# Weight sums in place, PSUM bank pairs by role and a later gate in a two-layer transformer block on one Trainium2 core

## The chip, the core and the metric

The kernel runs on one core of one Trainium2 chip. The metric is the device time of the whole program in microseconds. The engines are named as in the profile: PE (TensorE, with PEld for its weight loads), DVE (VectorE, "Vector"), ACT (ScalarE), POOL (GpSimd) and SP (SyncE, which issues the transfers).

## What is computed

The reference runs two layers on 256 tokens of width 1024. Each layer has a feed-forward block, a mixer and a second feed-forward block; a norm ends the program. So four feed-forward blocks run in all, and the change lies in them and in the first mixer.

```python
def swiglu(x, w_gate, w_up, w_down):          # 1024 -> 2816 -> 1024
    return (jax.nn.silu(x @ w_gate) * (x @ w_up)) @ w_down
...
for layer in range(DEPTH):                     # DEPTH = 2
    x = x + 0.5 * swiglu(rms_norm(x, ffn_norm[layer, 0]), ...)
    h = rms_norm(x, mix_norm[layer])
    x = x + (hybrid_ab_mixer(h, ...) if layer % 2 == 0 else short_conv_mixer(h, ...))
    x = x + 0.5 * swiglu(rms_norm(x, ffn_norm[layer, 1]), ...)
return rms_norm(x, final_norm)
```

All data are float32. The hybrid mixer (layer 0) has a gated unit and causal attention with four heads; the other is a short convolution.

## The kernel before

Precision is kept by splitting every weight and every activation into a rounded high part and a low rest (whi and wlo, hi and lo). A product is three matmuls: high by high, and the two mixed ones.

**The weight stream.** The class `Weights` holds the list of weight chunks (`Item`s) in the order of use. Sync loads a chunk into one of five raw slots (L71). ACT writes whi (`high`, L95), Vector writes wlo = raw - whi (`low`, L100); each has four buffers. `low` also returns the raw slots that an item drops and starts the next loads. An item may ask for sums of raw chunks first, which Vector computes (`sums`, L91). `next`, called once per chunk by the code of the matmuls, runs `catch_up`: high parts are issued three chunks ahead, low parts two, and sums one further than the high parts. Each engine works its own list strictly in the order in which the code issues it, so an instruction that waits holds up all behind it.

**A feed-forward block** (`ffn`). First a pair of 256 columns of gate and up is "opened" (`open_pairs`, transposed output, banks named by `ps()`); ACT and Vector take it out of PSUM (`added`, L418 and L424, tiles ev_g and ev_u). In block 1 the pair is opened by code of its own. Then 26 steps follow, one per chunk, in the order of the string `ORDER`; I number them from 0. "n" is a step of a plain unit: 512 columns of gate and up, four chunks, 24 matmuls each; gate goes to one pair of banks, up to another, then silu (L545) and the product v (`times`, L542). "s" is a step of a sum unit: 12 matmuls. A sum unit computes the two products of 512 columns for both token halves with seven half-size products instead of eight, from sums of the weight chunks b11, b12, b21, b22 and sums of activations (`Sums.make`, tiles xs and xp). Plain steps are 0, 1, 3, 5, 7, 10, 12, 14, 16, 18, 21 and 25. The results v (or r of a sum unit) are turned by four PE transposes each (`turned`, L533) into one misc bank and split into hx (L405 on ACT, L408 on Vector); the second turn of a unit uses the same bank as the first, so it waits for the first one's hx. Between the steps hooks run: the norm's column matmuls (L372), ten small Vector operations from rs_v (L309) to diag (L377), the broadcast matmul (L382, rbc) and the gate of the opened pair (`gated`, L430, L522, L523, hx). After the loop come the down products (L282, L284). In block 4 they are natural products into `ps(0)`.

**PSUM.** There are three pairs of banks, ps0 to ps2 (`ps`), and two single banks (`misc`). `ps()` takes the next pair in turn. In the block's loop the pairs are fixed: gate ps1, up ps2, sum units ps0. Which pairs the opened products hold depends on the turn: ps1 and ps2 in blocks 1 and 4, ps0 and ps1 in blocks 2 and 3.

**Sum unit before.** Its seven items are, in order: b11; t = b11 - b12, with t in a raw slot that loads nothing; b11 = b11 - (b12 + b22), with both sums asked for by this item; b22; b12 + b22; b21; b11 + b21. In the program that is four sums in three places. In the loop's order the sums are issued in steps 0, 2 (two of them) and 9, and for the second unit in steps 13, 15 (two) and 20.

**Block 1's hooks.** Step 8 loads small tensors, step 15 computes the angles (15 small Vector operations, L686 to L706), step 22 computes sines and then `turn_small`: the gains' transpose (L257), Vector's copy of it (gains_mix, L259) and four transposes of w_s (L731) into the same bank.

Of the kernel before, what the change touches and what calls it, by code (L numbers as in the profile page):

```python
# [10 lines left out]
F32 = mybir.dt.float32  # L11
# [36 lines left out]
class Weights:  # L48
# [6 lines left out]
    def __init__(self, nc, pool, items):  # L55
        self.nc, self.pool, self.items = nc, pool, items
        self.src = [load for item in items for load in item.loads]
        self.shapes = {name: tuple(src.shape) for name, src in self.src if src is not None}
        self.loaded = self.summed = self.highs = self.lows = self.used = 0
        self.raw, self.parts, self.queue = {}, {}, []  # L60
        self.free = [f"raw{i}" for i in range(RAW_BUFS)]

    def load_piece(self, i, s, e):
        name, src = self.src[i]
        if name not in self.raw:
            tag = self.free.pop(0)
            shape = list(src.shape) if src is not None else [P, 4, 512]
            self.raw[name] = self.pool.tile(shape, F32, tag=tag, bufs=1, name="raw"), tag
            self.loaded = i + 1
        if src is not None:  # L70
            self.nc.sync.dma_start(self.raw[name][0][:, s:e], src[:, s:e])  # L71

    def load(self):
        while self.loaded < len(self.src) and self.free:
            src = self.src[self.loaded][1]
            self.load_piece(self.loaded, 0, 0 if src is None else src.shape[1])

# [58 lines left out]
def block_kernel(ctx: ExitStack, tc: tile.TileContext, a, out):  # L136
# [35 lines left out]
    def sum_unit(g, u, c):  # L172

        b11, b12, b21, b22, t = (next(names) for _ in range(5))
        lo, hi = slice(0, 4), slice(4, 8)
        yield Item([(b11, u[:, lo, c])], b11, drop=[])
        yield Item([(b12, g[:, lo, c]), (t, None)], t, [(t, b11, b12, ALU.subtract)])
        yield Item([(b22, g[:, hi, c])], b11, [(b12, b12, b22, ALU.add), (b11, b11, b12, ALU.subtract)], drop=[])
        yield Item([], b22)
        yield Item([], b12)  # L180
        yield Item([(b21, u[:, hi, c])], b21, drop=[])
        yield Item([], b11, [(b11, b11, b21, ALU.add)], drop=[b11, b21])
# [259 lines left out]

    def open_pairs(xs, order=range(KB), mm=mm_t, banks=None):

        tiles = [(W.next(later=i > 0), ps(banks and banks[i])) for i in range(2)]
        W.flush(W.used + 1)
# [4 lines left out]

    def t_pair(xs, mid=None, mm=None, i=None):
        w, p = W.next(), ps(i)
        for b in range(2):
# [8 lines left out]

    def out_projection(h, norm, order, banks=None):
        ys = open_pairs(h, order, banks=banks)
        W.catch_up()
# [44 lines left out]
    def ffn(norm, nxt, hooks=None, opened=None, squares=None):  # L511
# [57 lines left out]
        def summed(f):  # L569

            p, b = ps(0), misc(0)
            a, c = p[:, 0], p[:, 1]
# [45 lines left out]
        g0, u0 = (added(p, tag) for p, tag in zip(pairs, ("ev_g", "ev_u")))  # L618
        W.catch_up()
        steps = {"n": (i for j in (0, 2, 4) for i in plain(2 + 4 * j)),  # L620
                 "s": (i for j in (1, 3) for i in summed(2 + 4 * j))}

        def scale():
            norm.broadcast()
            gated(g0, u0)

        if opened:
            head = {0: [squares, xs.gained], 1: [norm.column, lambda: xs.make(0)], 2: [scale], 3: [lambda: xs.make(1)]}
        else:
            head = {0: [norm.column], 1: [scale]}  # L630
        head[5], head[6] = [lambda: xs.make(2)], [lambda: xs.make(3)]
# [94 lines left out]
    def turn_small():  # L726

        small["turn"]()
        wp = misc(1)
# [76 lines left out]
    norm = nxt  # L806


    def project(i, mid=None):
        p = ps(i)  # L810
        for c in range(2):
# [29 lines left out]
    def heads_t(xs, name, i):  # L841
        r, p = big(name), ps(i)
        for t, x in enumerate(xs):
# [34 lines left out]
    def scores():  # L878
        s0p, s1p = misc(), ps(1)
        pr0, pr1 = big("prob0"), big("prob1")  # L880
# [40 lines left out]

    u_ps = t_pair(norm.x, scores, mm_s, 0)
    u0 = gate(u_ps)
    normalize()
    v_ps = project(2)
    v_sb = scaled(v_ps, "v")
# [8 lines left out]
    for c in range(2):  # L935
        nc.vector.tensor_copy(pt_a[c][:, :, :P], p[:, c * S:(c + 1) * S].rearrange("p (h k) -> p h k", h=2))
    p = ps(0)
    for c in range(2):
# [10 lines left out]
    def mix():  # L949

        ms, m_ps = big("mixed"), ps(2)
        for c in range(2):
# [210 lines left out]
```

## Time and profile before

| what | us |
|---|---|
| median of 3 runs | 976.96 (976.76 to 978.97) |
| profiled execution | 977.29 |
| its span | 975.5 |
| mean granted PE clock, share of full | 0.986 |
| PE busy | 933.1 |
| DVE busy | 729.3 |
| ACT busy | 504.2 |
| the four loops of steps, from their first matmul | 20.8 to 152.0, 315.5 to 430.6, 506.8 to 621.3, 790.1 to 907.3 |

The times of the profile are microseconds from the start of the span, which is the time from the first to the last instruction. The profiled execution's own time holds the span and what lies around it. In a row of waits the numbers are the total, how often and the longest. In a row of the timeline they are start and length; a bracket gives the engine's idle time ahead of it and what ended it.

### The profile page before, as it was taken

How to read it: one execution, taken by the hardware profiler on the slowest of the kernel's cores; microseconds unless marked ns; L12 is line 12 of the kernel's file. 1: busy time of each engine (PE TensorE's matmuls, PEld its weight loads, DVE VectorE, ACT ScalarE, POOL GpSimd, SP SyncE). 2: the span in 40 equal slices, each digit the busy share in tenths (PEclk: the TensorE clock that was granted, in tenths of full speed). 3: DMA queues.
4: the chain of work that ended last, by engine and by line, in shares of the span. 5: the costliest groups of instructions: out<-in, count | busy, mean ns of one | idle time of the engine just before them, and what ended most of it. 6: DMA issues, size and time to landing. Idle time of an engine off the chain costs nothing.

```text
span 975.5 us, 11868 instructions
## 1 busy us (share of the span) xinstructions
PE 933.1 (96%) x4916; PEld 795.6 (82%) x4916; DVE 729.3 (75%) x740; ACT 504.2 (52%) x510; POOL 3.2 (0%) x9
## 2 busy tenths in 40 slices
PE   8899899999998999999999999999999989999997
PEld 7678678888987788788877878888999877878786
DVE  6888886566768889885768898755587779989562
ACT  6566454454747465463454556444444555646342
POOL 0000000000000000000000000000000000000000
PEclk9989999999999999999999999999999999999999
DMA  9446475646352465676534565847446525746511
GB/s 326 149 154 215 161 236 175 216 162 227 111 181 87 130 215 182 201 243 194 171 112 142 181 215 173 270 162 232 156 154 195 197 69 169 261 147 241 209 65 43
DMA packets 121169, 173.82 MB, mean 178 GB/s; under 512 B 3408, under 2 KB 69532, under 8 KB 121116
## 3 DMA queue, kind: packets, MB, share of 16 engines
q1 hardware_dynamic: 120780, 172.53, 53.2%
q8 instruction: 38, 0.62, 0.3%
q10 hardware_dynamic: 336, 0.54, 0.2%
q14 instruction: 15, 0.12, 0.0%
HBM read 172.01 MB, written 1.05 MB: 177 GB/s over the span
## 4 chain that ended last, share of the span: by engine, by line
PE 70%; DVE 15%; DMA 6%; ACT 4%; issue 3%; SPq 0%; DVEq 0%; ACTq 0%
PE ps L282 12%; PE ps L297 11%; PE ps L296 11%; PE ps L298 11%; PE ps L284 6%; DMA raw<-in_ffn_w_gate 6%; DVE wlo L100 5%; DVE raw L91 4%; PE ps L290 3%; PE ps L291 3%; PE ps L292 3%; PE misc L298 2%; PE misc L296 2%; PE misc L297 2%; PE misc L533 2%
## 5 line engine op out<-in xcount | busy, mean ns | idle before, releaser
L95 ACT ACTIVATE whi<-raw 128x2048 fp32r<-128x2048 f32 (+2 forms) x196 | 354.3, 1823 | 186.0 <-PE ps L298 53.3
L100 DVE TENSOR_TENSOR wlo<-raw,whi 128x2048 fp32r<-128x2048 f32 (+2 forms) x196 | 422.8, 2175 | 22.4 <-ACT whi L95 22.3
L296 PE MATMUL ps<-whi,x 128*128 128x512 f32 x512 | 206.1, 403 | 8.3 <-DVE ev_u L424 4.8
L297 PE MATMUL ps<-wlo,x 128*128 128x512 f32 x512 | 204.1, 399 | 7.8 <-DVE wlo L100 7.5
L298 PE MATMUL ps<-whi,x 128*128 128x512 f32 x512 | 203.6, 398 | 0.0
L282 PE MATMUL ps<-hx,whi 128*128 128x512 f32 x528 | 166.9, 397 | 2.3 <-DVE v L542 2.3
L297 PEld LDWEIGHTS ps<-wlo,x 128*128 128x128 f32 x512 | 98.4, 192 | 31.5 <-DVE wlo L100 11.7
L296 PEld LDWEIGHTS ps<-whi,x 128*128 128x128 f32 x512 | 98.6, 193 | 29.7 <-DVE ev_u L424 5.5
L284 PEld LDWEIGHTS ps<-hx,wlo 128*128 128x128 f32 x528 | 99.2, 188 | 23.4
L298 PEld LDWEIGHTS ps<-whi,x 128*128 128x128 f32 x512 | 98.2, 192 | 20.9
L284 PE MATMUL ps<-hx,wlo 128*128 128x256 f32 x528 | 104.0, 278 | 0.0
L282 PEld LDWEIGHTS ps<-hx,whi 128*128 128x128 f32 x528 | 80.4, 189 | 2.7 <-issue 2.7
L91 DVE TENSOR_TENSOR raw<-raw 128x2048 f32<-128x2048 f32 x32 | 73.2, 2288 | 9.5 <-DMA raw<-in_ffn_w_gate 9.1
L390 DVE SCALAR_TENSOR_TENSOR xT<-ps,xT 128x512 f32<-128x512 f32 x40 | 27.4, 690 | 69.1 <-PE ps L284 61.3
L290 PE MATMUL ps<-x,whi 128*128 128x256 f32 x224 | 64.0, 286 | 0.0
L291 PE MATMUL ps<-x,whi 128*128 128x256 f32 x224 | 63.4, 283 | 0.0
L292 PE MATMUL ps<-x,wlo 128*128 128x256 f32 x224 | 63.4, 283 | 0.0
L408 DVE TENSOR_TENSOR hx<-misc,hx 128x512 fp32r<-128x512 f32 x40 | 27.5, 688 | 36.5 <-ACT hx L405 36.5
L274 PE MATMUL ps<-x,whi 128*128 128x512 f32 x128 | 45.5, 399 | 0.0
L291 PEld LDWEIGHTS ps<-x,whi 128*128 128x128 f32 x224 | 43.0, 192 | 0.0
L290 PEld LDWEIGHTS ps<-x,whi 128*128 128x128 f32 x224 | 43.0, 192 | 0.0
L292 PEld LDWEIGHTS ps<-x,wlo 128*128 128x128 f32 x224 | 43.0, 192 | 0.0
(244 smaller groups left out, 1133.9 us busy)
## 6 DMA issues: line engine op xcount, KB each, us to landing
raw<-in_ffn_w_gate SPq DMA_DIRECT2D x43, 1024.0 KB, 5.1
raw<-in_ffn_w_up SPq DMA_DIRECT2D x43, 1024.0 KB, 5.2
raw<-in_ffn_w_down SPq DMA_DIRECT2D x34, 1024.0 KB, 5.4
raw<-in_conv_w_in SPq DMA_DIRECT2D x12, 1024.0 KB, 5.2
raw<-in_hyb_w_in SPq DMA_DIRECT2D x10, 1024.0 KB, 6.4
raw<-in_ffn_w_down SPq DMA_DIRECT2D x12, 768.0 KB, 4.8
raw<-in_hyb_w_out SPq DMA_DIRECT2D x4, 1024.0 KB, 5.2
raw<-in_conv_w_out SPq DMA_DIRECT2D x4, 1024.0 KB, 5.9
```

The lines of the kernel that those rows point to most:

```text
L91: self.nc.vector.tensor_tensor(self.raw[dst][0], self.raw[x][0], self.raw[y][0], op=op)
L95: self.nc.scalar.activation(self.part(i, "whi")[:, s:e], self.tile(i)[:, s:e], AF.Copy)
L100: self.nc.vector.tensor_tensor(lo[:, s:e], raw[:, s:e], hi[:, s:e].bitcast(F32), op=ALU.subtract)
L274: nc.tensor.matmul(dst, whi, x, start=start, stop=False, skip_group_check=True)
L282: nc.tensor.matmul(dst, ws[i][0], xs[i], start=start and i == 0, stop=False, skip_group_check=True)
L284: nc.tensor.matmul(dst[:, :S], ws[i][1], xs[i][:, :S], start=False, stop=stop and i == n - 1, skip_group_check=True)
L290: nc.tensor.matmul(dst[:, :S], whi, x[:, :S], start=start, stop=False, skip_group_check=True)
L291: nc.tensor.matmul(dst[:, :S], whi, x[:, S:], start=False, stop=False, skip_group_check=True)
L292: nc.tensor.matmul(dst[:, :S], wlo, x[:, :S], start=False, stop=stop, skip_group_check=True)
L296: nc.tensor.matmul(dst, xhi, whi, start=start, stop=False, skip_group_check=True)
L297: nc.tensor.matmul(dst, xhi, wlo, start=False, stop=False, skip_group_check=True)
L298: nc.tensor.matmul(dst, xlo, whi, start=False, stop=stop, skip_group_check=True)
```

## The change

Five edits go together.

- *Sums in place.* t has no slot. Item 2 is b11 = b11 - b12, in place; item 3 subtracts b22 from that, in place; item 5 computes b12 + b22. Each item asks for one sum at most. b22 is dropped with b12 behind item 5, one or two steps later than before.
- *Bank pairs by role.* `ffn` notes the turn before it opens its pair (`last`). Gate takes pair `last`, up `last + 2`, sum units `last + 1` (all modulo 3); the opened pair held `last + 1` and `last + 2`. Behind the loop the turn is set so that the first down product takes `last`, gate's pair. The first mixer names its pairs relative to the turn as well (`hps`), and the v projection takes role 1 in place of pair 2.
- *The gate of the opened pair* runs behind step 2 in blocks 2 to 4; it ran behind step 1, together with the broadcast. In block 1 it stays behind step 2.
- *Block 1's hooks.* The angles go from step 15 to 13, the gains' transpose and its copy from step 22 to 21.
- `W` no longer knows items without a source.

```diff
     def sum_unit(g, u, c):
 
-        b11, b12, b21, b22, t = (next(names) for _ in range(5))
+        b11, b12, b21, b22 = (next(names) for _ in range(4))
         lo, hi = slice(0, 4), slice(4, 8)
         yield Item([(b11, u[:, lo, c])], b11, drop=[])
-        yield Item([(b12, g[:, lo, c]), (t, None)], t, [(t, b11, b12, ALU.subtract)])
-        yield Item([(b22, g[:, hi, c])], b11, [(b12, b12, b22, ALU.add), (b11, b11, b12, ALU.subtract)], drop=[])
-        yield Item([], b22)
-        yield Item([], b12)
+        yield Item([(b12, g[:, lo, c])], b11, [(b11, b11, b12, ALU.subtract)], drop=[])
+        yield Item([(b22, g[:, hi, c])], b11, [(b11, b11, b22, ALU.subtract)], drop=[])
+        yield Item([], b22, drop=[])
+        yield Item([], b12, [(b12, b12, b22, ALU.add)], drop=[b12, b22])
         yield Item([(b21, u[:, hi, c])], b21, drop=[])
...
                     if i == 0:
-                        p[j] = ps(1 + j)
+                        p[j] = ps((last + 2 * j) % 3)
...
-            p, b = ps(0), misc(0)
+            p, b = ps((last + 1) % 3), misc(0)
...
+        last = turns["ps"]
         xs = Sums(norm)
         pairs = opened or open_pairs(norm.x)
...
         W.catch_up()
+        turns["ps"] = (last + 2) % 3
...
-        def scale():
-            norm.broadcast()
+        def first():
             gated(g0, u0)
 
         if opened:
-            head = {0: [squares, xs.gained], 1: [norm.column, lambda: xs.make(0)], 2: [scale], 3: [lambda: xs.make(1)]}
+            head = {0: [squares, xs.gained], 1: [norm.column, lambda: xs.make(0)], 2: [norm.broadcast, first],
+                    3: [lambda: xs.make(1)]}
         else:
-            head = {0: [norm.column], 1: [scale]}
+            head = {0: [norm.column], 1: [norm.broadcast], 2: [first]}
...
     def turn_small():
 
-        small["turn"]()
         wp = misc(1)
...
-    ffn(norm, nxt, {8: load_small, 15: angles, 22: start_hybrid, 23: tables}, [p for _, p in opened], squares)
+    ffn(norm, nxt, {8: load_small, 13: angles, 21: lambda: small["turn"](), 22: start_hybrid, 23: tables}, [p for _, p in opened], squares)
...
+    def hps(i):
+        turns["ps"] = (last + 1 + i) % 3
+        return ps(turns["ps"])
...
-    v_ps = project(2)
+    v_ps = project(1)
...
-        ms, m_ps = big("mixed"), ps(2)
+        ms, m_ps = big("mixed"), hps(1)
...
-    u_ps = t_pair(norm.x, mix_and_attend, mm_s, 1)
+    u_ps = t_pair(norm.x, mix_and_attend, mm_s, hps(2))
+    turns["ps"] = (last + 3) % 3
```

Two places show what moves. The first is Vector's list in block 2, from the split low of step 3's chunk to the product v of the first plain unit. This is before:

```order
L100 TENSOR_TENSOR wlo_2556<-raw,whi_2503 128x2048
L430 TENSOR_TENSOR ev_g<-ev_g,rbc 128x512
L430 TENSOR_TENSOR ev_u<-ev_u,rbc 128x512
L523 TENSOR_TENSOR ev_u<-ev_g,ev_u 128x512
L100 TENSOR_TENSOR wlo_2599<-raw,whi_2554 128x2048
L408 TENSOR_TENSOR hx_2593<-ev_u,hx_2593 128x2x256
L91 TENSOR_TENSOR raw<-raw 128x2048 x2
L100 TENSOR_TENSOR wlo_2621<-raw,whi_2597 128x2048
L100 TENSOR_TENSOR wlo_2655<-raw,whi_2619 128x2048
L583 TENSOR_TENSOR r<-r,ps 128x512
L100 TENSOR_TENSOR wlo_2672<-raw,whi_2653 128x2048
L542 SCALAR_TENSOR_TENSOR v<-ps,rstd,s 128x512 x2
```

The five wlo rows are the splits of steps 3 to 7. The gate (ev_g, ev_u) stands ahead of step 4's split, and both sums behind it. This is the list now, from step 4's split on (lines of the changed file are three or four lower):

```order
L96 TENSOR_TENSOR wlo_2592<-raw,whi_2553 128x2048
L87 TENSOR_TENSOR raw<-raw 128x2048
L426 TENSOR_TENSOR ev_g<-ev_g,rbc 128x512
L426 TENSOR_TENSOR ev_u<-ev_u,rbc 128x512
L519 TENSOR_TENSOR ev_u<-ev_g,ev_u 128x512
L96 TENSOR_TENSOR wlo_2616<-raw,whi_2590 128x2048
L404 TENSOR_TENSOR hx_2612<-ev_u,hx_2612 128x2x256
L96 TENSOR_TENSOR wlo_2651<-raw,whi_2614 128x2048
L579 TENSOR_TENSOR r<-r,ps 128x512
L96 TENSOR_TENSOR wlo_2668<-raw,whi_2649 128x2048
L87 TENSOR_TENSOR raw<-raw 128x2048
L538 SCALAR_TENSOR_TENSOR v<-ps,rstd,s 128x512 x2
```

Step 4's split and one sum now stand ahead of the gate; the other sum stands between step 7's split and v.

The second place is Vector's list in block 2 from step 14's v to the two hx rows of the first sum unit. Before:

```order
L542 SCALAR_TENSOR_TENSOR v<-ps,rstd,s 128x512 x2
L100 TENSOR_TENSOR wlo_2959<-raw,whi_2921 128x2048
L91 TENSOR_TENSOR raw<-raw 128x2048 x2
L408 TENSOR_TENSOR hx_2983<-misc,hx_2983 128x2x256
L100 TENSOR_TENSOR wlo_2988<-raw,whi_2957 128x2048
L408 TENSOR_TENSOR hx_3022<-misc,hx_3022 128x2x256
```

Now, and on to the sum of step 18:

```order
L538 SCALAR_TENSOR_TENSOR v<-ps,rstd,s 128x512 x2
L96 TENSOR_TENSOR wlo_2957<-raw,whi_2919 128x2048
L87 TENSOR_TENSOR raw<-raw 128x2048
L404 TENSOR_TENSOR hx_2978<-misc,hx_2978 128x2x256
L96 TENSOR_TENSOR wlo_2983<-raw,whi_2955 128x2048
L404 TENSOR_TENSOR hx_3017<-misc,hx_3017 128x2x256
L96 TENSOR_TENSOR wlo_3022<-raw,whi_2981 128x2048
L579 TENSOR_TENSOR r<-r,ps 128x512
L96 TENSOR_TENSOR wlo_3039<-raw,whi_3020 128x2048
L87 TENSOR_TENSOR raw<-raw 128x2048
```

One of the two sums ahead of the first hx is gone from there, and stands six rows further on, behind step 20's split.

More of the change, by code (lines that the diff above doesn't have):

```diff
@@ L57, in __init__ @@
         self.src = [load for item in items for load in item.loads]
-        self.shapes = {name: tuple(src.shape) for name, src in self.src if src is not None}
         self.loaded = self.summed = self.highs = self.lows = self.used = 0
@@ L66, in load_piece @@
             tag = self.free.pop(0)
-            shape = list(src.shape) if src is not None else [P, 4, 512]
-            self.raw[name] = self.pool.tile(shape, F32, tag=tag, bufs=1, name="raw"), tag
+            self.raw[name] = self.pool.tile(list(src.shape), F32, tag=tag, bufs=1, name="raw"), tag
             self.loaded = i + 1
-        if src is not None:
-            self.nc.sync.dma_start(self.raw[name][0][:, s:e], src[:, s:e])
+        self.nc.sync.dma_start(self.raw[name][0][:, s:e], src[:, s:e])
     def load(self):
         while self.loaded < len(self.src) and self.free:
-            src = self.src[self.loaded][1]
-            self.load_piece(self.loaded, 0, 0 if src is None else src.shape[1])
+            self.load_piece(self.loaded, 0, self.src[self.loaded][1].shape[1])
     def tile(self, i):
@@ L441, in t_step, with open_pairs @@
                 mm(p[:, b], wcol(w, k, b), x, start, stop)
-    def open_pairs(xs, order=range(KB), mm=mm_t, banks=None):
-        tiles = [(W.next(later=i > 0), ps(banks and banks[i])) for i in range(2)]
+    def open_pairs(xs, order=range(KB), mm=mm_t):
+        tiles = [(W.next(later=i > 0), ps()) for i in range(2)]
         W.flush(W.used + 1)
@@ L450, in open_pairs, with t_pair @@
         return [p for _, p in tiles]
-    def t_pair(xs, mid=None, mm=None, i=None):
-        w, p = W.next(), ps(i)
+    def t_pair(xs, mid=None, mm=None, p=None):
+        w, p = W.next(), p or ps()
         for b in range(2):
@@ L462, in t_pair, with out_projection @@
         return p
-    def out_projection(h, norm, order, banks=None):
-        ys = open_pairs(h, order, banks=banks)
+    def out_projection(h, norm, order):
+        ys = open_pairs(h, order)
         W.catch_up()
@@ L804, in block_kernel @@
     nxt = Norm(lambda d: gain("mix", d))
-    ffn(norm, nxt, {8: load_small, 15: angles, 22: start_hybrid, 23: tables}, [p for _, p in opened], squares)
+    ffn(norm, nxt, {8: load_small, 13: angles, 21: lambda: small["turn"](), 22: start_hybrid, 23: tables}, [p for _, p in opened], squares)
     norm = nxt
+    last = turns["ps"]
+    def hps(i):
+        turns["ps"] = (last + 1 + i) % 3
+        return ps(turns["ps"])
     def project(i, mid=None):
-        p = ps(i)
+        p = hps(i)
         for c in range(2):
@@ L841, in heads_t @@
     def heads_t(xs, name, i):
-        r, p = big(name), ps(i)
+        r, p = big(name), hps(i)
         for t, x in enumerate(xs):
@@ L878, in scores @@
     def scores():
-        s0p, s1p = misc(), ps(1)
+        s0p, s1p = misc(), hps(1)
         pr0, pr1 = big("prob0"), big("prob1")
@@ L920, in gated @@
         return split(mixed[c], f"c{c}")
-    u_ps = t_pair(norm.x, scores, mm_s, 0)
+    u_ps = t_pair(norm.x, scores, mm_s, hps(0))
     u0 = gate(u_ps)
     normalize()
-    v_ps = project(2)
+    v_ps = project(1)
     v_sb = scaled(v_ps, "v")
@@ L936, in block_kernel @@
         nc.vector.tensor_copy(pt_a[c][:, :, :P], p[:, c * S:(c + 1) * S].rearrange("p (h k) -> p h k", h=2))
-    p = ps(0)
+    p = hps(0)
     for c in range(2):
@@ L986, in mix_and_attend @@
         attend()
-    u_ps = t_pair(norm.x, mix_and_attend, mm_s, 1)
+    u_ps = t_pair(norm.x, mix_and_attend, mm_s, hps(2))
+    turns["ps"] = (last + 3) % 3
     cat = gated(0, u0) + gated(1, gate(u_ps)) + heads
     nxt = Norm(lambda d: gain("ffn", KB + d))
-    turns["ps"] = 0
-    out_projection(cat, nxt, (0, 1, 4, 5, 6, 7, 2, 3), (0, 2))
+    out_projection(cat, nxt, (0, 1, 4, 5, 6, 7, 2, 3))
     norm = nxt
```

## Prediction

> **What bounds the kernel now.** I read the page first, then the waits of PE, then windows around those waits, then Vector's timeline where PE waited for it. The page says how much there is to win at most.
>
> ```profile
> span 975.5 us, 11868 instructions
> PE 933.1 (96%) x4916; PEld 795.6 (82%) x4916; DVE 729.3 (75%) x740; ACT 504.2 (52%) x510; POOL 3.2 (0%) x9
> ```
>
> PE is busy for 933.1 of 975.5 us, and the change takes no matmul away. So it can only shorten PE's 42 us of idle time and the matmuls that run at a lower clock. The waits of PE (total, times, longest) name the idle time:
>
> ```profile
> PE misc L533 <- DVE hx L408: 10.2, 6, 3.1
> PE ps L297 <- DVE wlo L100: 7.5, 5, 3.8
> PE ps L296 <- DVE ev_u L424: 4.8, 2, 2.9
> PE ps L296 <- DVE ev_g L424: 3.5, 2, 2.5
> PE ps L282 <- DVE v L542: 2.3, 2, 1.2
> PE misc L731 <- DVE gains_mix L259: 2.1, 1, 2.1
> PE misc L382 <- DVE diag L377: 1.4, 1, 1.4
> ```
>
> Every large wait is for Vector (DVE), and all lie in the four feed-forward blocks. The windows show what follows a wait (columns: stretch, its length, busy time of PE, PEld, DVE, ACT, POOL, then PE's granted clock, DMA share, GB/s):
>
> ```profile
> 104.00:107.40 3.40, 0.36 (x2) 0.00 (x0) 3.37 (x4) 0.51 (x1) 0.00 (x0) 1.00 0.32 125
> 107.80:111.20 3.40, 3.40 (x11) 2.73 (x10) 3.02 (x14) 3.28 (x3) 0.00 (x0) 0.50 0.00 0
> 132.60:135.00 2.40, 0.29 (x2) 0.00 (x1) 2.40 (x4) 1.40 (x2) 0.00 (x0) 1.00 0.00 0
> 135.10:138.50 3.40, 3.40 (x11) 2.83 (x12) 1.98 (x1) 3.06 (x5) 0.00 (x0) 0.51 0.88 282
> 312.60:315.50 2.90, 0.04 (x1) 0.00 (x0) 2.20 (x5) 2.59 (x4) 0.00 (x0) 1.00 0.00 0
> 316.00:319.40 3.40, 3.40 (x10) 2.65 (x9) 3.40 (x2) 2.12 (x2) 0.00 (x0) 0.51 0.16 17
> 341.90:392.60 50.70, 50.60 (x227) 41.40 (x227) 45.29 (x33) 28.85 (x24) 0.00 (x0) 1.00 0.61 207
> 392.60:394.60 2.00, 0.18 (x1) 0.00 (x0) 2.00 (x3) 0.51 (x1) 0.00 (x0) 1.00 0.00 0
> 394.70:398.10 3.40, 3.40 (x17) 2.89 (x18) 3.40 (x3) 3.40 (x3) 0.00 (x0) 1.00 0.09 15
> ```
>
> Idle stretches of 2.4 to 3.4 us (104.0, 132.6, 312.6) are each followed by 3.4 us at a clock of 0.50 to 0.51, which costs half of it, 1.7 us. The 2.0 us at 392.6 cost nothing more. From 341.9 to 392.6 PE runs without a gap: 227 instructions in 50.7 us, 0.223 us each, so a plain step (24 matmuls) takes 5.4 us and a step of a sum unit (12) 2.7.
>
> **Block 2, the model for three blocks.** Its rows of Vector's timeline (start, length, instruction, and in brackets the idle time before it) carry the sum:
>
> ```profile
> 315.38 4.49 DVE L100 TENSOR_TENSOR wlo<-raw,whi 128x2048 fp32r<-128x2048 f32 x2
> 323.23 0.16 DVE L309 TENSOR_SCALAR rs_v<-misc 128x2 f32<-128x2 f32 x1 [1.16 <-PE misc L372]
> 329.69 0.69 DVE L430 TENSOR_TENSOR ev_g<-ev_g,rbc 128x512 f32<-128x512 f32 x1 [1.81 <-ACT rbc L384]
> 331.64 0.69 DVE L523 TENSOR_TENSOR ev_u<-ev_g,ev_u 128x512 f32<-128x512 f32 x1 [0.65 <-ACT ev_g L522]
> 335.05 4.61 DVE L91 TENSOR_TENSOR raw<-raw 128x2048 f32<-128x2048 f32 x2
> 339.58 4.49 DVE L100 TENSOR_TENSOR wlo<-raw,whi 128x2048 fp32r<-128x2048 f32 x2
> 347.46 1.41 DVE L542 SCALAR_TENSOR_TENSOR v<-ps,rstd,s 128x512 f32<-128x512 f32 x2 [0.51 <-PE ps L298]
> 368.13 2.28 DVE L100 TENSOR_TENSOR wlo<-raw,whi 128x2048 fp32r<-128x2048 f32 x1
> 389.37 4.62 DVE L91 TENSOR_TENSOR raw<-raw 128x2048 f32<-128x2048 f32 x2 [1.59 <-DMA raw<-in_ffn_w_gate]
> 393.91 0.68 DVE L408 TENSOR_TENSOR hx<-misc,hx 128x512 fp32r<-128x512 f32 x1
> ```
>
> *The banks.* Step 0 now writes the third bank pair, whose last reader was long done, so PE starts it at 312.6 and not at 315.5, and the half clock from 316.0 has no cause left. That is 2.9 + 1.7 = 4.6 us on PE. It is not what the block gains, because Vector is late next.
>
> *Vector's chain, up to step 12.* From 315.38 to the end of v at 348.8 Vector does the same instructions before and after, in another order (one of the three sums in it moves behind the split low of step 7). It idles 1.16 + 1.81 + 0.65 + 0.51 = 4.1 us in between. The first goes, because PE's column matmuls come about 4.6 us earlier, when Vector still has its first sum to do (ends 322.0). The second goes, because the gate now stands a step later and a split and a sum lie in its place. The fourth goes with PE's lead. The silu round trip of 0.65 stays. So v ends 3.4 us earlier, at 345.4. PE reaches the transposes that need v (behind step 6) after four plain steps (21.6), three of a sum unit (8.1) and about 1.8 for the norm's matmuls and their wait for diag (an estimate, from the 1.4 that L382 waited in block 1): 312.6 + 31.5 = 344.1. It waits 1.2 us there, a new wait. Behind it in PE's queue stand the matmuls of step 7, so everything after is late by it; nobody but hx waits for the transposes themselves. Each of the steps 5 and 12 wants its split low at about the time Vector ends it; step 12's ends at 370.4 - 3.4 = 367.0, and PE would want it at about 366.0 (345.4, three sum-unit and two plain steps of 18.9, and eight transposes of about 0.2). So at step 12 the block is 3.4 us ahead, as much as Vector and not as much as PE.
>
> *The sum that leaves step 15.* At 389.37 Vector waited 1.59 for a transfer and then did two sums, and hx at 393.91 came behind them, while PE stood from 392.6. Now the transfer starts two steps sooner, because no raw slot is given to t (Sync issues its transfers in the same order as before), and one sum of 2.3 stands there. hx ends at 394.6 - 3.4 - 1.6 - 2.3 = 387.3. PE gets there at 392.6 - 3.4 = 389.2. The wait of 2.0 goes whole: 5.4 us ahead. The other sum now stands at step 18; Vector is 7.3 us ahead by then and stays 5.0 ahead after it. PE, 5.4 ahead, has margins of about 1 us on its split lows there, so this is tight and I count no wait.
>
> *The end of the loop.* The first down product (L282) took the pair that v is read from, and waited 1.2 us; now it takes the gate's pair, which is free. The transposes behind it will wait for hx instead, as they do in block 1. I count half, 0.7 with rounding.
>
> Block 2: 3.4 + 2.0 + 0.7 = 6.1 us.
>
> **Blocks 3 and 4** have the same instructions. From the chain that ended last:
>
> ```profile
> 506.02 0.69 DVE ev_u L424
> 530.27 2.30 DVE wlo L100
> 584.68 0.61 DVE hx L408
> 789.49 0.61 DVE ev_g L424
> 813.64 2.29 DVE wlo L100
> 867.95 0.61 DVE hx L408
> ```
>
> In block 2 step 5's split low ended at 341.8, 26.4 us after ev_u's add (315.4). In block 3 it is 532.6 - 506.7 = 25.9, in block 4, with ev_u's add 0.6 behind ev_g's, 815.9 - 790.7 = 25.2. Afterwards it should be the same length in all three, so the head brings 0.5 and 1.2 less: 2.9 and 2.2. Step 15's sum brings 2.0 and 1.9. The loop's end brings 0.7 in block 3 and nothing in block 4, whose down products start on another pair. Together 5.6 and 4.1 us.
>
> **Block 1.** Its Vector rows:
>
> ```profile
> 48.21 2.28 DVE L100 TENSOR_TENSOR wlo<-raw,whi 128x2048 fp32r<-128x2048 f32 x1
> 58.92 1.41 DVE L542 SCALAR_TENSOR_TENSOR v<-ps,rstd,s 128x512 f32<-128x512 f32 x2 [0.77 <-PE ps L298]
> 102.18 4.62 DVE L91 TENSOR_TENSOR raw<-raw 128x2048 f32<-128x2048 f32 x2 [1.54 <-DMA raw<-in_ffn_w_gate]
> 106.71 0.68 DVE L408 TENSOR_TENSOR hx<-misc,hx 128x512 fp32r<-128x512 f32 x1
> 107.31 0.16 DVE L686 CAST posf<-pos_i 128x2 f32<-128x2 int32 x1
> ...
> 110.27 0.18 DVE L706 TENSOR_SCALAR ang_c<-ang_c 128x32 f32<-128x32 f32 x1
> ```
>
> One sum ahead of the gate, where there were two, lets step 5's split at 48.21 end 2.3 us sooner, at 48.2, which shortens PE's longest wait (3.8) to 1.5. But the second sum comes back ahead of v: only the 0.77 is saved, v ends at 59.6, PE has been there since 48.2 + 5.1 + 2.7 = 56.0, and the new wait of 3.6 us brings a half clock of its own. At step 12 PE meets Vector again, and the block is 0.7 ahead. Further on, the angles' fifteen small operations (107.31 to 110.45, 3.1 us) go ahead of step 14's split low, and hx moves from 106.71 by 0.7 + 1.5 + 2.3 - 3.1 = 1.4 us. That leaves PE a wait of about 1.3 where it had 3.1, too short for the half clock at 107.8, so 1.4 + 1.7 = 3.1. The gains' transpose (its loads stay at step 8) moves a step ahead of the four w_s transposes, and Vector's copy of it moves with it, past one split and one add; with a sum-unit step of 2.7 us between, the copy is done when PE arrives: the 2.1 us at 132.6 and the 1.7 behind them go. Block 1: 3.1 + 3.8 = 6.9, with the 0.7 inside the 3.1.
>
> **A rule against the trace.** Idle stretches of 2.4 and 2.9 us were followed by the half clock here. The Trainium skill (TensorE: Matmul & The Clock Gate, Part 1: The HAM clock gate) says that the gate falls to half rate after at least one idle window of about 3.4 us. By it the 2.4 us at 132.6 would not be the cause of what follows, and the sum would be 1.7 us less, 21.0; the trace's rows decide.
>
> **Edits that cost nothing.** The hybrid's new banks put v's projection on the pair that the scores are read from; all other reuses are as old as before. Nothing in the trace shows that wait, so it is bounded by 0 and by a step's 2.7 us, and I take 0, since PE has half a projection between.
>
> **The sum.** 6.9 + 6.1 + 5.6 + 4.1 = 22.7 us. The profiled execution took 977.29 us, 1.8 over its span and 0.33 over the median of 976.96. 977.29 - 22.7 - 0.33 = 954.3.
>
> **Rivals.** *All of the waits go.* If Vector keeps up, the listed waits (31.8 us) go, and with them, as an estimate, five half clocks like the three above (8.5): 977 - 40 = 937. Against it, the third sum ahead of v. Chance 0.10. *The heads bring nothing.* If Vector's idle gaps at the heads only move behind the later gate, 3.4 + 2.9 + 2.2 + 0.7 = 9.2 fall away: 963.5. For it, Vector's order is tight at every step. Chance 0.18. *It does not do what it says.* The waits return one for one, behind the sums at steps 5 and 18: 977. Chance 0.04. *Slower: the raw slots.* b12 and b22 are held until the fifth item of a unit, so the plain chunks behind them are loaded one or two steps later. If ACT then finds one not landed, PE loses up to a short step of 2.7 us, at three chunks in each of four blocks: 32 us, against 22.7 won: 987. It decides when a transfer's slack falls below a step; in block 2's order these chunks still have two or more steps. Chance 0.04.
>
> **How the numbers follow.** My forecast has 0.64. I predict 954.3 us. The range takes in the second rival with 2 us beyond and half the way to the first: 943 to 966. A measurement here tells 0.3%, 2.9 us. Faster by more: the forecast and the first two, 0.92. Within: 0.04. Slower: 0.04.
>
> **What would show it.** Right: no wait of L296 for ev_g or ev_u and full clock at the heads of blocks 2 to 4; a new wait of about 1 us of L533 for v (3 to 4 in block 1); hx of step 15 done before PE's transposes in blocks 2 to 4; no wait for gains_mix. Wrong: waits of ACT's split for transfers in the middle of a block, waits for wlo in steps 18 to 25, or a half clock behind step 6 in blocks 2 to 4.

## The result, and the profile after

The changed kernel takes 951.11 us (median of 4 runs, 950.75 to 953.38), the kernel before 977.05 on the same chip: a ratio of 0.9735 (95% interval 0.9716 to 0.9755). The profiled execution took 951.3 us. 954.3 was predicted.

The page's head and the busy times of the kernel after:

```profile
span 949.6 us, 11856 instructions
PE 923.6 (97%) x4916; PEld 788.6 (83%) x4916; DVE 728.3 (77%) x740; ACT 505.1 (53%) x510; POOL 2.0 (0%) x9
```

PE issues the same 4916 matmuls, busy for 9.5 us less: its mean granted clock rose from 0.986 to 0.997, so less of the work runs at half clock. Vector works as long as before, in a span that is 26 us shorter. The waits of PE after (total, times, longest):

```profile
PE ps L293 <- DVE wlo L96: 4.7, 5, 1.6
PE misc L529 <- DVE hx L404: 3.6, 5, 1.1
PE misc L378 <- DVE diag L373: 3.0, 3, 1.4
PE misc L529 <- DVE v L538: 2.9, 4, 2.3
```

No wait for ev_g, ev_u or gains_mix is left, and hx fell from 10.2 to 3.6. The wait of L529 for v is new. The windows after (same columns as before) show the one long wait that is left, and the heads of blocks 2 to 4:

```profile
56.00:58.50 2.50, 0.40 (x2) 0.00 (x0) 2.50 (x2) 0.00 (x0) 0.00 (x0) 1.00 0.57 138
58.90:62.30 3.40, 3.07 (x10) 2.46 (x10) 2.70 (x4) 2.37 (x3) 0.00 (x0) 0.60 0.41 159
304.60:308.00 3.40, 3.40 (x17) 2.84 (x16) 2.70 (x6) 2.66 (x4) 0.00 (x0) 1.00 0.27 106
490.00:493.40 3.40, 3.40 (x17) 2.85 (x16) 3.14 (x4) 3.40 (x5) 0.00 (x0) 1.00 0.00 0
766.40:769.80 3.40, 3.40 (x17) 2.82 (x16) 2.70 (x6) 2.62 (x4) 0.00 (x0) 1.00 0.26 99
```

The heads now run at full clock without a gap. The first row is block 1's wait for v (2.3 us without a matmul), the second the slower clock behind it. Block 2's rows of Vector's timeline, up to v, and those of step 12 and of the turn behind step 16:

```profile
307.81 4.49 DVE L96 TENSOR_TENSOR wlo<-raw,whi 128x2048 fp32r<-128x2048 f32 x2
...
314.54 0.15 DVE L305 TENSOR_SCALAR rs_v<-misc 128x2 f32<-128x2 f32 x1
...
321.42 2.29 DVE L87 TENSOR_TENSOR raw<-raw 128x2048 f32<-128x2048 f32 x1
323.63 0.68 DVE L426 TENSOR_TENSOR ev_g<-ev_g,rbc 128x512 f32<-128x512 f32 x1
...
325.02 0.69 DVE L519 TENSOR_TENSOR ev_u<-ev_g,ev_u 128x512 f32<-128x512 f32 x1
...
333.44 2.28 DVE L87 TENSOR_TENSOR raw<-raw 128x2048 f32<-128x2048 f32 x1
335.64 1.40 DVE L538 SCALAR_TENSOR_TENSOR v<-ps,rstd,s 128x512 f32<-128x512 f32 x2
...
356.30 2.29 DVE L96 TENSOR_TENSOR wlo<-raw,whi 128x2048 fp32r<-128x2048 f32 x1
...
376.08 2.29 DVE L87 TENSOR_TENSOR raw<-raw 128x2048 f32<-128x2048 f32 x1
378.29 0.68 DVE L404 TENSOR_TENSOR hx<-misc,hx 128x512 fp32r<-128x512 f32 x1
```

None of the rows from 307.81 to v has idle time in brackets; before there were four gaps, 4.1 us. Counted from the first row, v starts after 27.8 us (before: 347.46 - 315.38 = 32.1), step 12's split after 48.5 (52.8) and the turn's hx after 70.5 (78.5).

Where PE's matmuls of the same number stand in the two traces gives the gain of each block: 7.8, 6.8, 6.4 and 5.0 us, 26.0 together; the spans differ by 25.9. Predicted were 6.9, 6.1, 5.6 and 4.1.

### The profile page after: what moved, and what is told of

The parts are those of the page before. It is cut to its first block, busy times and chain, and to the rows that moved or that the text cites. A ratio compares the mean times of both kernels' runs of the same rounds, so it can differ in the third digit from the quotient of the medians.

```text
span 949.6 us, 11856 instructions
## 1 busy us (share of the span) xinstructions
PE 923.6 (97%) x4916; PEld 788.6 (83%) x4916; DVE 728.3 (77%) x740; ACT 505.1 (53%) x510; POOL 2.0 (0%) x9
## 4 chain that ended last, share of the span: by engine, by line
PE 65%; DVE 23%; ACT 6%; issue 4%; DMA 1%; SPq 0%; DVEq 0%; ACTq 0%
PE ps L278 12%; DVE wlo L96 10%; PE ps L293 9%; PE ps L294 9%; PE ps L292 8%; PE ps L280 6%; DVE raw L87 4%; PE ps L286 3%; PE ps L287 3%; PE ps L288 3%; PE ps L270 2%; PE misc L294 2%; PE misc L292 2%; PE misc L293 2%; ACT whi L91 2%
## 5 line engine op out<-in xcount | busy, mean ns | idle before, releaser
L293 PE MATMUL ps<-wlo,x 128*128 128x512 f32 x512 | 200.7, 392 | 4.7 <-DVE wlo L96 4.7
L292 PE MATMUL ps<-whi,x 128*128 128x512 f32 x512 | 203.0, 396 | 0.0
L294 PE MATMUL ps<-whi,x 128*128 128x512 f32 x512 | 200.2, 391 | 0.0
L294 PEld LDWEIGHTS ps<-whi,x 128*128 128x128 f32 x512 | 96.4, 188 | 20.4
L292 PEld LDWEIGHTS ps<-whi,x 128*128 128x128 f32 x512 | 96.6, 189 | 19.7
```

What stands on the lines that cost most here:

```text
L292: nc.tensor.matmul(dst, xhi, whi, start=start, stop=False, skip_group_check=True)
L293: nc.tensor.matmul(dst, xhi, wlo, start=False, stop=False, skip_group_check=True)
L294: nc.tensor.matmul(dst, xlo, whi, start=False, stop=stop, skip_group_check=True)
```

## The experiments

Two theories were set against each other first. *Vector's chain*: PE meets Vector again at steps 5 and 12 and at the turns, so a block wins what Vector's list wins, and a wait of PE between is free. *PE's waits*: each wait with its half clock costs what it lasts. Every edit is to the changed kernel, and its time is compared with 951.1 us. The runs were made on several chips, on which the kernel before took 976.19 to 977.21 us, so a difference of less than about 1 us between two runs tells nothing. Ratios are to the kernel before on the same chip. What a block loses or gains is read from matmuls of the same number in two traces, from the end of one loop to the end of the next.

**old_banks.** The old fixed pairs of banks.

```
-                        p[j] = ps((last + 2 * j) % 3)
+                        p[j] = ps(1 + j)
...
-            p, b = ps((last + 1) % 3), misc(0)
+            p, b = ps(0), misc(0)
...
-        turns["ps"] = (last + 2) % 3
```

> The changed kernel, with the bank pairs of the steps fixed as before (gate ps1, up ps2, sum units ps0) and no reset of the turn behind the loop. Vector theory (the blocks' heads are set by Vector's list up to step 12): PE starts step 0 only when the opened pair has been taken out, and at half clock; Vector idles about 1.2 us again before rs_v; PE reaches step 12 about 1.9 us later in blocks 2 and 3, 1.3 in block 4, and the loop's end loses 0.7 twice: 951.1 + 6.5 = 957.6. PE theory (PE's waits and half clocks count one for one): 4.6 + 3.7 + 4.2 for the heads and 1.4 for the ends: 965. In both, waits of the first matmul for ev_g or ev_u come back, four of them, and half clock behind three.

958.91 us (958.62 to 959.14), ratio to before 0.9818 [0.9798, 0.9838]. The waits that come back on PE, and two windows at the head of block 2:

```profile
PE ps L292 <- DVE ev_u L420: 5.3, 2, 3.1
PE ps L292 <- DVE ev_g L420: 3.7, 2, 2.5
PE ps L278 <- DVE v L538: 2.3, 2, 1.2
```

```profile
305.00:308.20 3.20, 0.50 (x2) 0.46 (x3) 2.50 (x5) 3.10 (x4) 0.00 (x0) 1.00 0.07 26
308.30:311.70 3.40, 3.40 (x10) 2.68 (x9) 3.40 (x2) 2.00 (x2) 0.00 (x0) 0.53 0.17 19
```

At its head block 2 loses 3.3 us up to its first matmul and 1.7 in the half clock, 5.0 together; by step 12 2.5 of it are left, and at the block's end, with the wait for v, 3.1. Blocks 3 and 4 lose 3.1 and 1.8. The banks are worth 7.8 us, nearer to Vector's chain (6.5) than to PE's waits (14).

**gate_step1.** The opened pair's gate back at step 1.

```
-            head = {0: [norm.column], 1: [norm.broadcast], 2: [first]}
+            head = {0: [norm.column], 1: [norm.broadcast, first]}
```

> The changed kernel, with the gate of the opened pair behind step 1 again in blocks 2 to 4. Vector theory: with the early start of step 0 the broadcast lands at 318.2 in block 2, and Vector is busy with a split until 319.1, so it does not wait for it; at most the silu's table load of block 2 comes back (0.6): 951.1 to 951.7, the same. Rival (the later gate is what removed the 1.8 us that Vector waited for rbc): 1.8 in each of three blocks, 956.5, and the wait for rbc is back in the trace.

951.15 us (950.6 to 954.0), 0.9746 [0.9717, 0.9775]: the same as with the later gate. With the banks early the norm's broadcast is there in time, and the gate no longer waits for it:

```profile
319.08 0.69 DVE L426 TENSOR_TENSOR ev_g<-ev_g,rbc 128x512 f32<-128x512 f32 x1
```

So of the 1.81 us that the prediction gave to the later gate, the gate itself earns nothing: with the earlier banks the wait is gone without it.

**old_sums.** A sum's slot t of its own, and both sums at one chunk, as before.

```
+        b11, b12, b21, b22, t = (next(names) for _ in range(5))
...
+        yield Item([(b12, g[:, lo, c]), (t, None)], t, [(t, b11, b12, ALU.subtract)])
+        yield Item([(b22, g[:, hi, c])], b11, [(b12, b12, b22, ALU.add), (b11, b11, b12, ALU.subtract)], drop=[])
```

> The changed kernel, with the sums as before: t in a raw slot of its own, two sums asked for by item 3. Vector theory: nothing is lost up to step 12 in blocks 2 to 4, because Vector's list there is as long as now; the wait for hx behind step 16 comes back with about 1.8 us in each, block 1 loses about 1 by step 12 and 3 to 4 behind step 16 with its half clock: 951.1 + 10 = 961. PE theory: the waits for wlo and hx come back as they were, 2.8 + 6.6, and five half clocks of 1.7 less those of the heads: 964 to 966.

980.88 us (978.39 to 984.86, 10 runs), 1.0049 [1.0034, 1.0063]: slower than the kernel before, and 15 to 20 us from what either theory said. Vector's timeline in block 2, and PE's two largest waits over the whole trace:

```profile
329.83 4.62 DVE L90 TENSOR_TENSOR raw<-raw 128x2048 f32<-128x2048 f32 x2 [3.01 <-DMA raw<-in_ffn_w_gate]
334.37 0.69 DVE L429 TENSOR_TENSOR ev_g<-ev_g,rbc 128x512 f32<-128x512 f32 x1
...
336.37 2.28 DVE L99 TENSOR_TENSOR wlo<-raw,whi 128x2048 fp32r<-128x2048 f32 x1
```

```profile
PE ps L296 <- DVE wlo L99: 18.4, 6, 4.4
PE misc L532 <- DVE hx L407: 13.2, 8, 4.8
```

The sums wait 3.0 us for the transfer of b22, the gate and the next split low are queued behind them, and PE stands. The windows of the same stretch:

```profile
333.90:338.60 4.70, 0.43 (x2) 0.01 (x1) 4.60 (x6) 2.74 (x3) 0.00 (x0) 0.93 0.00 0
338.90:345.70 6.80, 6.80 (x18) 5.35 (x19) 5.36 (x4) 4.77 (x5) 0.00 (x0) 0.57 0.51 160
```

A wait of 4.4 us is followed by 6.8 us at a mean clock of 0.57. Both theories fell here: they left out the weight transfers. The next two runs take this apart.

**slot_held.** Sums in place and one to a chunk, but each sum unit also holds an empty slot t, as the old sums did. Nothing reads or writes the slot.

```
+        b11, b12, b21, b22, t = (next(names) for _ in range(5))
...
+        yield Item([(b12, g[:, lo, c]), (t, None)], b11, [(b11, b11, b12, ALU.subtract)], drop=[t])
```

> The changed kernel, with one sum to a chunk in place as now, but item 2 also holds a raw slot that nothing is loaded into, as t did. It tells apart what cost so much with the old sums. Transfer theory (t's slot makes b22's transfer late, Vector waits 3.0 us for it at step 2, and the later gate stands behind that): Vector is about 3 us later at step 12 in blocks 2 to 4, block 1 loses 1: 961. Sum theory (the second sum in one place cost all of the 30 us): 951 to 953.

963.81 us (962.72 to 964.35), 0.9878 [0.9861, 0.9896]. The sum at step 2 of block 2 waits as long as in old_sums:

```profile
326.44 2.29 DVE L90 TENSOR_TENSOR raw<-raw 128x2048 f32<-128x2048 f32 x1 [2.99 <-DMA raw<-in_ffn_w_gate]
```

Sync's rows with the issue of that transfer (b22, the first of the two in the row), in this run and then in the changed kernel:

```profile
321.28 0.92 SPq L70 DMA_DIRECT2D raw<-in_ffn_w_gate  x2
```

```profile
310.16 9.42 SPq L68 DMA_DIRECT2D raw<-in_ffn_w_gate  x2
```

With the slot held b22 is issued 11.4 us behind the block's first row (309.88 in this trace), in the changed kernel 2.4 behind it (307.81); in both it lands 5.0 to 5.1 us after its issue. So the slot that t holds is one that the next chunk's transfer waits for. Over the whole trace the sums wait 17.9 us for transfers, against 2.2 in the changed kernel, while ACT's splits wait 10.8 in both. The slot alone costs 12.7 us of the 30 that old_sums loses: in the traces 2.1 in block 1 and 3.0 to 3.1, as much as the sum waits, in each of the others. There are not more half clocks: the one in block 1 is gone, and one in block 4 is new (0.52 from 802.2 to 805.6).

**old_sums_gate1.** The old sums, and the gate back at step 1 too, so that of the change only the banks and the hooks of block 1 are left.

```
-            head = {0: [norm.column], 1: [norm.broadcast], 2: [first]}
+            head = {0: [norm.column], 1: [norm.broadcast, first]}
```

> The old sums, with the gate behind step 1 as before; so of the change only the bank pairs and block 1's hooks are left. Transfer theory: the gate is done while Vector would wait for b22, so step 5's split ends about 2 us sooner than with the old sums and the later gate, and PE's wait of 4.5 there falls to about 2.5, with half of its half clock: 980.9 - 3 times 3.7 = 970. If the gate's place makes no difference, as it made none with the new sums: 981.

972.49 us (969.61 to 975.38, 10 runs), 0.9964 [0.9949, 0.9979]. The gate now stands ahead of the sums, and their wait has shrunk from 3.01 to 0.42 us:

```profile
325.68 0.68 DVE L429 TENSOR_TENSOR ev_g<-ev_g,rbc 128x512 f32<-128x512 f32 x1
...
330.99 4.62 DVE L90 TENSOR_TENSOR raw<-raw 128x2048 f32<-128x2048 f32 x2 [0.42 <-DMA raw<-in_ffn_w_gate]
```

So the later gate, worth nothing beside the new sums (951.15 against 951.11), costs 8.4 us beside the old ones. And the banks with the hooks, without the new sums, bring 3.7 us (976.23 to 972.49), 0.4%, where the whole change brings 2.65%.

**sums_late.** If the sum ahead of v holds PE up in block 1, issue each sum at its step's end, behind v and the gate.

```
-        self.sums(self.used + AHEAD + 1)
...
+            W.sums(W.used + AHEAD + 1)
```

> The changed kernel, with each step's sum issued at the end of the step, behind v and the hooks, where it stood ahead of them. Vector theory: the waits for v behind step 6 go (2.5 with a half clock in block 1, 0.4 elsewhere), the waits for diag too, but Vector's list up to step 12 is as long as before, so step 12's split ends when it did and the blocks gain nothing there; block 1 may gain 1 behind step 16: 950 to 951.1. PE theory: the waits count, 2.9 for v, 1.6 for diag and 1.7 of half clock: 945.

958.77 us (958.51 to 959.17), 0.9813 [0.9792, 0.9834]: 7.7 us slower than the changed kernel, where both theories had expected no loss. The wait for v did go (0.3 us), but ACT's split of the next chunk waits for the sum (two rows of ACT's timeline in block 2):

```profile
340.14 1.92 ACT L91 ACTIVATE whi<-raw 128x2048 fp32r<-128x2048 f32 x1 [3.02 <-DVE raw L87]
...
394.72 3.73 ACT L91 ACTIVATE whi<-raw 128x2048 fp32r<-128x2048 f32 x2 [3.02 <-DVE raw L87]
```

ACT's part of hx is queued behind such splits, Vector's part waits for it (in block 2 6.3 us in all, 4.2 in the changed kernel), and the waits of PE for split lows rise:

```profile
PE ps L292 <- DVE wlo L96: 7.4, 9, 1.3
PE misc L292 <- DVE wlo L96: 5.6, 4, 1.9
```

So the place ahead of v isn't idle: a sum issued a little later holds up ACT's split, and what is queued behind it.

**fill_wait.** Does the half clock behind block 1's wait for v cost anything? Eight extra matmuls of the identity, into the bank that the transposes then overwrite, keep PE busy there; nothing reads them.

```
+                if not room.get("filled"):
+                    room["filled"] = True
+                    for _ in range(FILL):
+                        nc.tensor.matmul(m[:, :P], ident, ident, start=True, stop=True)
```

> The changed kernel, with eight matmuls of the identity on itself in block 1 ahead of the first transposes; the transposes overwrite their result. They fill PE's wait for v. The windows should show full clock from 59 to 62, where it was half. Vector theory: step 12's split ends at 80.9 all the same, so at most 0.4 of the 1.7 us is kept: 950.7 to 951.1. PE theory: 1.7 is won: 949.4.

951.27 us (950.86 to 951.38), 0.9735 [0.9718, 0.9752]: no change. The same two windows, and the waits for split lows and v:

```profile
56.00:58.50 2.50, 2.01 (x18) 1.78 (x17) 2.50 (x3) 0.00 (x0) 0.00 (x0) 1.00 0.69 178
58.90:62.30 3.40, 3.16 (x16) 2.65 (x17) 2.70 (x4) 2.58 (x3) 0.00 (x0) 1.00 0.33 130
```

```profile
PE ps L294 <- DVE wlo L97: 5.9, 7, 1.6
PE misc L534 <- DVE v L543: 1.3, 5, 0.5
```

The clock stays at 1.00 and PE is ahead, only to wait 1.2 us more for split lows. A half clock inside PE's slack against Vector costs nothing here, as Vector's chain says.

**turn_22.** The gains' transpose back ahead of the four w_s transposes.

```
+        small["turn"]()
...
-    ffn(norm, nxt, {8: load_small, 13: angles, 21: lambda: small["turn"](), 22: start_hybrid, 23: tables}, ...
+    ffn(norm, nxt, {8: load_small, 13: angles, 22: start_hybrid, 23: tables}, ...
```

> The changed kernel, with the gains' transpose at step 22 again, right ahead of the four w_s transposes. Mine: the wait for gains_mix comes back with about 2 us, long enough for a half clock of 1.7: 954.9. Rival (Vector is ahead enough by then to copy at once, so only the round trip of about 0.6 shows and no half clock follows): 951.7.

955.21 us (954.09 to 955.62), 0.9779 [0.9758, 0.9799]: 4.1 lost. The wait is back, 2.1 us long; PE is 2.5 late behind it, and 4.1 late behind the half clock that follows (0.57 from 132.8 to 136.2):

```profile
PE misc L729 <- DVE gains_mix L255: 2.1, 1, 2.1
```

These 4.1 us stay to the end of the program: here PE's wait counts in full, with its half clock, because PE doesn't meet Vector again in the rest of the block. The same trace has block 1's wait for v as before, 2.28 us long, and the clock behind it is full:

```profile
58.90:62.30 3.40, 3.20 (x16) 2.69 (x17) 2.70 (x4) 2.62 (x3) 0.00 (x0) 1.00 0.31 120
```

**angles_15.** The angles' small operations two steps later, out of the way of step 14's split and hx.

```
-    ffn(norm, nxt, {8: load_small, 13: angles, ...
+    ffn(norm, nxt, {8: load_small, 15: angles, ...
```

> The changed kernel, with block 1's angles at step 15 again. Mine: the fifteen small operations no longer stand ahead of step 14's split and of the first hx, so the waits of about 1.1 us at step 16 and 1.1 behind it go, and nothing comes in their place: 949.0. Rival (the move to step 13 was needed because they would hold up step 16's list): the same or slower, 951 to 953.

951.38 us (951.23 to 951.7), 0.9737 [0.972, 0.9755]: nothing, against an expected gain of 2. PE was 2.0 ahead at the turn behind step 16 and gave it back a little later, among others in waits of 0.8 us for hx and 0.6 for a split low. Vector's list is as long as it was; only the place of the wait moved.

**pool_sums.** The 32 sums on GpSimd, to take them off Vector.

```
-                self.nc.vector.tensor_tensor(self.raw[dst][0], self.raw[x][0], self.raw[y][0], op=op)
+                self.nc.gpsimd.tensor_tensor(self.raw[dst][0], self.raw[x][0], self.raw[y][0], op=op)
```

> The changed kernel, with the sums computed by GpSimd and not by Vector. Vector theory: each block's list on Vector is 8 sums of 2.2 us shorter, 3 of them ahead of step 12; where a GpSimd sum takes less than a step, PE's remaining waits for wlo, v and hx go, about 2 us a block: 943. If a GpSimd sum takes over about 5 us, ACT's split behind it is late and PE waits for it at each sum: 4 to 5 us at eight places in each block, slower than the kernel before.

1024.06 us (1021.04 to 1026.99), 1.048 [1.0449, 1.0511]. Groups of instructions (busy, mean ns of one, idle before it): the split low in the changed kernel, then in this run that split and the sum on GpSimd.

```profile
L96 DVE TENSOR_TENSOR wlo<-raw,whi 128x2048 fp32r<-128x2048 f32 (+2 forms) x196 | 422.9, 2175 | 23.3 <-ACT whi L91 23.1
```

```profile
L96 DVE TENSOR_TENSOR wlo<-raw,whi 128x2048 fp32r<-128x2048 f32 (+2 forms) x196 | 486.3, 2499 | 32.7 <-ACT whi L91 32.6
...
L87 POOL TENSOR_TENSOR raw<-raw 128x2048 f32<-128x2048 f32 x32 | 162.5, 5088 | 726.3 <-DVE rs_v L305 507.4 <-DVE wlo L96 89.2 <-DMA raw<-in_ffn_w_gate 88.5
```

A sum takes 5.09 us there on average, almost two steps of a sum unit, and it stops Vector. The 0.32 us by which the mean of the split lows grew are not spread over them: of the 174 splits of 128x2048, 158 take 2.2 to 2.3 us as ever, and 16 take 5.7 to 6.7. Each of the 16 began while a sum ran and ended 2.15 us behind that sum's end, about the usual length of a split. Even this small instruction in block 2, elsewhere 0.17 us long, ends only with the sum beside it (a row of GpSimd's timeline, then one of Vector's):

```profile
332.97 4.59 POOL L87 TENSOR_TENSOR raw<-raw 128x2048 f32<-128x2048 f32 x1 [198.58 <-DVE rs_v L305]
```

```profile
333.14 4.44 DVE L307 TENSOR_SCALAR rs_h<-rs_h 128x2 int32<-128x2 int32 x1
```

Instructions with an operand in PSUM (hx at 123.33, r at 369.46) took 0.69 and 0.68 us within a sum, as outside. Vector is relieved of 32 sums of 2.29 us, 73 us, and still is busy for 775.5 us instead of 728.3. The second branch of the expectation had the sign and one cause (ACT's splits wait 68.7 us for sums), but not the size (4 to 5 us at 32 places), and it didn't name Vector's stops.

**lows_late.** If Vector's order sets the time, the splits that PE wants first should go first. The low parts of the chunks of the gained input (xp 1 to 3) and of each unit's second hx are put behind the next weight split; the code that reads them is as before.

```
-            nc.vector.tensor_tensor(r[:, 1], src, r[:, 0].bitcast(F32), op=ALU.subtract)
+            def low():
+                nc.vector.tensor_tensor(r[:, 1], src, r[:, 0].bitcast(F32), op=ALU.subtract)
+
+            if i:
+                W.afterwards(low)
+            else:
+                low()
...
-                h[f + 2 * q:f + 2 * q + 2] = split(m, f + 2 * q)
+                h[f + 2 * q:f + 2 * q + 2] = split(m, f + 2 * q, q == 1)
```

> The changed kernel, with the low parts of xp 1 to 3 and of each unit's second turned pair put behind the next chunk's split on Vector. Vector waits 0.7 us for ACT ahead of each xp and 1.3 ahead of that hx today; then it does a split meanwhile. Vector theory: its list up to step 12 gets about 3 us shorter, so PE's waits at step 12 (1.0) and step 9 (0.4) go, and about 1.4 us in each of blocks 2 to 4 and 1 to 2 in block 1 are won: 945.5. If PE's own work bounds the blocks: 951.

945.52 us (945.37 to 945.94), 0.9693 [0.9677, 0.9709]: 5.6 us better than the changed kernel, as expected. The waits of PE over the whole trace:

```profile
PE misc L378 <- DVE diag L373: 4.1, 4, 1.4
...
PE ps L293 <- DVE wlo L96: 2.3, 2, 1.6
PE misc L536 <- DVE v L545: 2.2, 5, 1.4
```

The waits for split lows are halved; those at step 12 of blocks 2 to 4 are gone. The four blocks win 2.9, 1.0, 1.0 and 1.0 in the trace, where 1 to 2 and three times 1.4 were expected: the sum was met better than its parts.

**lows_late15.** The same with the angles at step 15.

> The kernel with the late low parts, and the angles at step 15. Vector theory: with the slack won, the fifteen small operations fit behind the first hx, and block 1's waits at step 16 and behind it go: 1 us below the kernel with the late low parts, 944.5. If they only move the wait, as in the changed kernel: the same.

945.91 us (945.44 to 946.12), 0.9695 [0.9676, 0.9714]: the same as lows_late. The angles' place decides nothing in either order.

## Why the prediction was right, and where it was off

**The limit.** That a block wins what Vector's chain wins, and not what PE's waits last, held up to the last meeting of the two: old_banks keeps only 2.5 of 5.0 us by step 12, and fill_wait removes a half clock for nothing. Where PE doesn't meet Vector again, as behind the gains' transpose, the whole wait counts, and the prediction priced it so.

**Block 2, up to step 12.** 3.4 was predicted, 4.0 measured. The mis-sized step is "The silu round trip of 0.65 stays". It went too: in the timeline after, Vector has no idle bracket at ev_u's product (325.02). The wait wasn't the silu's round trip but a table load in front of it, the only one in the four loops; the rows of ACT's timeline in block 2, before and after:

```profile
329.68 1.28 ACT L522 ACT_TABLE_LOAD   x1
```

```profile
321.16 1.28 ACT L518 ACT_TABLE_LOAD   x1
```

Before, the load began together with Vector's scaling of ev_g (329.69), and the silu came behind both. Now it is over at 322.4, before that scaling starts (323.63). Vector's chain is 4.1 us shorter by its four idle gaps (4.25 by the starts of v). The new wait of L529 for v is 0.2 us and not 1.2: v ends 0.8 sooner than forecast, and the first transpose needs only the first of v's two instructions, so only the next one waits. Step 12's wait for its split low, 1.0 in the prediction, is 0.8.

**Blocks 3 and 4, up to step 12.** 2.9 and 2.2 were predicted, 3.7 and 3.1 measured. Here the working took the same 0.5 off twice. It read from the chain that the heads of these blocks were 0.5 and 1.2 us shorter before than block 2's, and subtracted this from 3.4. But 0.5 of each difference is the table load's wait, which blocks 3 and 4 didn't have (no bracket at 522.33 and 805.70) and which the 3.4 didn't contain. Their gaps on Vector before were 1.17, 1.81 and 0.52 us, and 0.56, 1.81 and 0.51: 3.5 and 2.9, close to what came.

**Block 2, the turn behind step 16.** 2.0 was predicted and 2.0 came: 4.0 ahead at step 12, 6.0 behind the turn. The sum at 376.08 shows no wait for a transfer. Blocks 3 and 4 brought 2.0 and 1.9 there, as predicted. **The loop's end** brought the 0.7 assumed in blocks 2 and 3: a wait for hx of 0.5 stands where 1.2 for v stood. The wait for diag, taken from another block, is 0.8. The first mixer's new banks cost next to nothing: PE is 7.8 us ahead when it begins and 7.7 at block 2's start.

**Block 1.** Every step has the predicted sign: 0.95 instead of 0.7 at step 12; a new wait for v of 2.3 us instead of 3.6, because PE came 0.4 us later and v 0.3 earlier than reckoned, and the first transpose needs only v's first half; 2.0 instead of 1.4 at the turn, with its 1.7 of half clock. The slower clock behind the wait for v was foreseen, but that it came is luck: in turn_22, slot_held and gate_step1 the same wait (2.28 to 2.30 us) is followed by full clock, and gate_step1 is no faster for it. The gains' transpose brought 3.7 in the traces against 3.8, and turn_22, which undoes it alone, loses 4.1.

**Which part carries it.** Here the working was too narrow, though the sum didn't suffer. It gave 1.81 us of Vector's idle time in block 2 to the later gate; gate_step1 shows that the gate earns nothing once the banks are early. It counted the slot that t no longer takes only at step 15 (1.6 of the 2.0). slot_held shows that the slot matters at step 2 as well: with the banks early and a sum ahead of the gate, Vector comes to the first sum with b22 13.6 us after the block's first row here (321.42 - 307.81) and not after 19.7 (335.05 - 315.38). With the slot held the sum has to wait 3.0 us for b22, to 16.6 us after that row (326.44 - 309.88). Before, the gate and the idle gaps ahead of the sums covered it: the row at 335.05 has no bracket. So the in-place sums are worth 21.3 us beside the new banks (972.49 - 951.15, both with the gate at step 1), the banks 7.8 and the gains' transpose 4.1, 33 together for a gain of 25.9. The parts aren't additive: the banks and the gains' transpose, worth 11.9 when each is undone alone, bring 3.7 without the new sums. The angles' new place brings nothing. The slot's 12.7 were measured beside the later gate; how much of the 21.3 it is with the gate at step 1, and how much the second sum in one place, stays open. Two sums in one place without holding the slot, with one more raw slot, wasn't tried.

**The rivals.** That all waits go (937) failed at step 5 of block 1 and at step 12, where PE still waits for split lows; lows_late takes 5.6 of the 14 us that were left. That the heads bring nothing (963.5) failed with the four idle gaps, and that the waits return one for one (977) with the waits of PE. The raw slots did decide something, but the other way round from the slower rival: the change frees a slot earlier on, and holding one costs 12.7 us, at the sum and not at ACT's split. One sign that was to show the prediction wrong did come: once in the middle of each block ACT's split now waits 1.2 to 1.8 us for a transfer (1.21 us ahead of 351.87 in block 2), where it didn't before. It is the chunk of step 12, and Vector comes to its split of it 2.5 us after ACT has ended (356.30, no bracket). So it costs nothing; in the four blocks 1.9 to 2.6 us are to spare.

**A rule against the trace.** In the changed kernel a wait of 2.3 us, up to 58.7, was followed by a clock of 0.60, and the 2.1 us of turn_22 by a loss of 1.6 more. By the Trainium skill's idle window of about 3.4 us (TensorE: Matmul & The Clock Gate, Part 1) neither should have happened. The traces speak for the shorter gap, and the sum without that rule was the nearer one. But the prediction's own reading, that 2.0 us cost nothing and 2.4 or more a half clock, was too simple as well; the last section has the gaps.

## What to carry to other kernels

When two engines take turns at being late, cost a change on the list of the second one: as long as the two meet again, removing a wait brings what the next engine's list gets shorter, and filling or moving the wait brings nothing. An earlier start only pays if what it uses arrives earlier too, so look at each transfer that the old wait covered; a slot that is held and delays a transfer is such a cost. Once the list is what limits, put first in it what the waiting engine reads first: that brought 5.6 us with no work taken away.

## What the hardware showed that was not expected

The slower clock comes behind short gaps, and not always. In the rows of PE, 1.97 us without a matmul up to 506.75 (before) brought a clock of 0.50, and 1.86 us up to 394.65 (before) left it at 1.00. 2.30 us up to 58.70 (after) brought 0.60, and 2.28 us at the same place in turn_22 left it at 1.00, as did 2.68 us up to 107.47 in slot_held. In old_sums 4.4 us brought 6.8 us at 0.57. So for gaps of about 2 to 2.7 us these traces give no rule by length alone, and the cost of a gap can be more than its own length.

An addition of two 128x2048 fp32 operands took 5.09 us on average on GpSimd and 2.29 on Vector, and most of Vector's instructions without an operand in PSUM that began beside it ended only behind it: 16 split lows took 5.7 to 6.7 us instead of 2.3. The Trainium skill (GPSIMD Engine Reference, Key points) says that the two engines share their interfaces to SBUF, with contention for Vector's instructions that are in a 2-port mode or have two SBUF inputs. The split lows, which have two such inputs, agree.
